# A two-layer encoder on one core: the Strassen subtractions of the down weights moved two chunks later and pinned behind a low part

## The chip, the core and the metric

The kernel runs on one core of a Trainium2 chip. The metric is the device time of one execution in microseconds (us); three runs of the kernel before took 2059.7, 2064.2 and 2067.19 us, with a median of 2064.2 us.

## The reference

The reference is an encoder trunk of two layers over 256 tokens of width 2048, all in float32. Each layer has a token mixer (attention in two variants) and a channel mixer, each between two RMS norms and added to the residual. The change lies in the channel mixer:

```python
def conv_glu(h, w_up, conv_w, conv_b, w_down):
    u = h @ w_up                                  # (256, 2048) @ (2048, 11264)
    gate, val = u[..., :D_FF], u[..., D_FF:]      # D_FF = 5632
    gate = depthwise_conv3(gate, conv_w, conv_b)
    return (jax.nn.gelu(gate, approximate=False) * val) @ w_down
```

## The kernel before

**Products in parts.** Every weight is multiplied as a high part plus a low part. A chunk is 128x1024 float32 numbers of a weight, 512 KB. SP loads it into one of four `raw` buffers (line 135). ACT casts it to the high part `whi` (line 157), DVE subtracts that from the chunk, which gives the low part `wlo` (line 152), and PE multiplies both with the activations. `whi` and `wlo` have five buffers each (`PARTED`), and `weights` makes the parts of a chunk two chunks before PE uses them and asks for its load up to four further ahead.

**Up projection** (`ffn`, `proj_t`). The 11264 columns are done in 11 groups of 512 gate columns and 512 value columns. Each half of a group takes 8 chunks; a chunk is eight pairs of a matmul with `whi` (line 231, 512 columns wide) and one with `wlo` (line 233, 256 wide). After each chunk `tick` advances the side jobs by one step each. When a half is done, ACT and DVE empty its four PSUM banks: for the gates lines 304, 305, 1112 to 1118 (convolution and gelu), for the values lines 304, 305, 1130, 1131 and 689, 690.

**Side job: block sums** (`block_sums`). The down projection later uses a Strassen form with seven products in place of eight, and for it needs differences of blocks of the down weights. From the second group on, a generator makes them for 20 pairs of weights in each layer, one pair (a *job*) in seven ticks, each tick being one step `q` from 0 to 6. A job loads its 128x2048 block in two halves (line 1154, at `q` 0 and 1) into one of two buffers that the jobs use in turn, makes three subtractions on DVE (`minus`, line 1141: one of 1024 columns and two of 512), and writes the two halves back to DRAM as `b` (line 1160). The wide subtraction stands at `q` 6 of the job itself, the two narrow ones at `q` 0 of the next job, and the write-back at its `q` 2 and 3. With the block sums running, seven chunks of up weights share the DMA with two loads and two write-backs of half a megabyte.

**What sets the order.** Nobody writes the order of an engine by hand here. When the program is built, each engine's instructions are put in a row that the engine then works off strictly in turn, waiting at each for its semaphores; within the dependences the building may move an instruction ahead of others. `issue_after`, which `behind` wraps, forbids that: what is issued inside it stays behind the named instruction. So a subtraction that waits for a load on DVE holds up every low part and every PSUM emptying behind it, and a load that waits on SP holds up every chunk behind it.

Of the kernel before, what the change touches and what calls it, by code (L numbers as in the profile page):

```python
# [58 lines left out]
class Model:  # L59
# [78 lines left out]
    def _split(self, i, parts=1, late=False):  # L138
        if i >= len(self.chunks) or i in self.made:
            return  # L140
        self._load(i)
        raw = self.loaded.pop(i)
        if i in self.spot:
            hi, lo = self.spot.pop(i)()
        else:
            hi = self.wp.tile([P, 1024], F32R, tag="whi", name="whi", bufs=PARTED)
            lo = self.wp.tile([P, 1024], F32R, tag="wlo", name="wlo", bufs=PARTED)
        n = raw.shape[-1] // parts

        def low(s=slice(0, raw.shape[-1])):  # L150
            nc = self.nc
            return nc.vector.tensor_tensor(out=lo[:, s], in0=raw[:, s], in1=hi[:, s].bitcast(F32), op=ALU.subtract)  # L152

        with self.behind(self.gate):
            for j in range(parts):
                s = slice(n * j, n * j + n)
                self.nc.scalar.copy(hi[:, s], raw[:, s])  # L157
                if not late:
                    low(s)
        self.made[i] = (hi, lo)  # L160
        if late:
            return low
# [972 lines left out]
    def block_sums(self, layer, sp):  # L1135

        nc, w = self.nc, self.a[f"w_down{layer}"]
        jobs = [(h, p) for h in range(2) for p in range(PAIRS[layer][h])]

        def minus(x, a, b, n=512):  # L1140
            nc.vector.tensor_tensor(out=x[:, a:a + n], in0=x[:, b:b + n] if n > 512 else x[:, a:a + n],  # L1141
                                    in1=x[:, a:a + n] if n > 512 else x[:, b:b + n], op=ALU.subtract)

        def half(x, i):
            return x[:, 1024 * i:1024 * i + 1024]

        old = None
        for n in range(len(jobs) + 1):
            job, new = (jobs[n] if n < len(jobs) else None), None
            for q in range(7):  # L1150
                if job and q == 0:
                    new = sp.tile([P, 2048], F32, tag=("st", "g_last")[n % 2], name="blocks", bufs=1)
                if job and q < 2:
                    nc.sync.dma_start(out=half(new, q), in_=half(w[job[0], job[1]], q))
                if old and q == 0:
                    minus(old[1], 1536, 512)
                    minus(old[1], 0, 1536)
                    kept = self.blocks[layer, *old[0]] = self.dram.tile([P, 2048], F32, name=f"b{layer}{old[0][0]}_{old[0][1]}")
                if old and q in (2, 3):
                    nc.sync.dma_start(out=half(kept, q - 2), in_=half(old[1], q - 2))  # L1160
                    if q == 3 and not job:
                        return
                if job and q == 6:
                    minus(new, 512, 1024, 1024)
                yield
            old = (job, new)

# [295 lines left out]
```

## Time and profile before

| | |
|---|---|
| median of three runs | 2064.2 us (2059.7 to 2067.19) |
| profiled execution | 2060.65 us, of which span 2058.9 us |
| PE matmul busy | 2037.1 us, 99% |
| PE weight loads busy | 1746.5 us, 85% |
| DVE busy | 1560.2 us, 76% |
| ACT busy | 1156.4 us, 56% |
| DMA, mean over the span | 248 GB/s |
| block sums run, layer 0 | from 343 to about 662 us |
| block sums run, layer 1 | from about 1339 to about 1663 us |

A line L231 of the profile is line 231 of the kernel; PEld is PE's loading of weights, SPq is SP's DMA queue. In a group of instructions the idle time is that of the engine just before them, with what ended it. The end of a matmul is modelled, so that a stall of PE can show partly as a longer matmul; the number of matmuls done in a stretch does not depend on that.

### The profile page before, as it was taken

What the parts mean: (1) busy time and instruction counts of PE and PEld (TensorE: products, weight loads), DVE (VectorE), ACT (ScalarE), POOL (GpSimd) and SP (SyncE); (2) the same over time, 40 slices, a digit from 0 to 9 for tenths busy, and PEclk for the clock granted to TensorE, in tenths of its full rate; (3) what the DMA queues carried; (4) which work ended last, traced back from release to release, by engine and by line L of the source; (5) the groups of instructions that cost most, each with busy time, mean ns of one, the idle gap of its engine ahead of it and who ended that gap; (6) DMA issues with size and microseconds to landing.
All of it is one profiled execution on the core that took longest, in us unless ns stands there. A gap on an engine that the chain in (4) does not pass through costs nothing.

```text
span 2058.9 us, 29791 instructions
## 1 busy us (share of the span) xinstructions
PE 2037.1 (99%) x10882; PEld 1746.5 (85%) x10882; DVE 1560.2 (76%) x2388; ACT 1156.4 (56%) x1817; POOL 0.2 (0%) x4
## 2 busy tenths in 40 slices
PE   9999999999999999999999999999999999999998
PEld 7888888888888888888878998888888888888886
DVE  6877757878777676977787875688887776688777
ACT  7655546554454555656665665565554555566664
POOL 0000000000000000000000000000000000000000
PEclk9999999999999999999999999999999999999999
DMA  9545567998998666788965445699899976668895
GB/s 334 180 152 161 166 198 245 318 321 308 331 305 310 208 182 192 237 295 280 317 204 180 141 129 170 207 321 334 311 316 306 316 252 195 192 198 303 271 321 197
DMA packets 145587, 509.75 MB, mean 248 GB/s; under 512 B 16160, under 2 KB 16672, under 8 KB 145440
## 3 DMA queue, kind: packets, MB, share of 16 engines
q1 hardware_dynamic: 145152, 507.58, 74.6%
q8 instruction: 85, 1.39, 0.3%
q14 instruction: 62, 0.51, 0.1%
q10 hardware_dynamic: 288, 0.28, 0.0%
HBM read 459.55 MB, written 48.23 MB: 247 GB/s over the span
## 4 chain that ended last, share of the span: by engine, by line
PE 87%; DVE 5%; DMA 4%; issue 2%; ACT 1%; SPq 0%; DVEq 0%; ACTq 0%
PE ps L231 25%; PE ps L233 12%; PE ps L216 8%; PE ps L214 8%; PE ps L215 8%; PE ps L1287 7%; PE ps L1286 7%; PE ps L1289 7%; DMA blocks<-in_w_down 3%; DVE wlo L152 2%; PE ps L641 1%; PE ps L300 1%; DMA raw<-in_w_up 1%; DVE blocks L1141 1%; PE ps L544 1%
## 5 line engine op out<-in xcount | busy, mean ns | idle before, releaser
L152 DVE TENSOR_TENSOR wlo<-raw,whi 128x1024 fp32r<-128x1024 f32 (+1 forms) x663 | 793.7, 1205 | 298.7 <-ACT whi L157 292.2
L157 ACT CAST whi<-raw 128x1024 fp32r<-128x1024 f32 (+1 forms) x663 | 682.9, 1036 | 520.7 <-PE ps L231 184.2
L231 PE MATMUL ps<-xhl,whi 128*128 128x512 f32 x2752 | 960.8, 396 | 0.0
L233 PE MATMUL ps<-xhl,wlo 128*128 128x256 f32 x2752 | 765.1, 280 | 8.7 <-DVE wlo L152 8.6
L231 PEld LDWEIGHTS ps<-xhl,whi 128*128 128x128 f32 x2752 | 516.5, 188 | 118.5
L233 PEld LDWEIGHTS ps<-xhl,wlo 128*128 128x128 f32 x2752 | 519.8, 189 | 15.6 <-DVE wlo L152 12.8
L1286 PE MATMUL ps<-whi,gh 128*128 128x512 f32 x440 | 171.5, 390 | 0.0
L1287 PE MATMUL ps<-whi,gl 128*128 128x512 f32 x440 | 171.4, 390 | 0.0
L1141 DVE TENSOR_TENSOR blocks<-blocks 128x512 f32<-128x512 f32 (+1 forms) x120 | 104.0, 867 | 85.1 <-DMA blocks<-in_w_down 55.3
L152 DVE TENSOR_TENSOR wlo<-raw_more,whi 128x1024 fp32r<-128x1024 f32 (+1 forms) x117 | 130.7, 1132 | 48.6 <-ACT whi L157 43.8
L157 ACT CAST whi<-raw_more 128x1024 fp32r<-128x1024 f32 (+1 forms) x117 | 113.2, 979 | 77.2 <-PE ps L1287 70.0
L1289 PE MATMUL ps<-wlo,gh 128*128 128x512 f32 x440 | 138.8, 390 | 0.0
L214 PE MATMUL ps<-whi,xhl 128*128 128x512 f32 x336 | 132.4, 395 | 1.7 <-ACT whi L157 1.7
L215 PE MATMUL ps<-wlo,xhl 128*128 128x512 f32 x336 | 131.6, 392 | 0.0
L216 PE MATMUL ps<-whi,xhl 128*128 128x512 f32 x336 | 131.1, 391 | 0.1
L304 ACT COPY gw<-ps 128x256 f32<-128x256 f32 x176 | 62.9, 368 | 93.7 <-DVE misc L305 43.2
L214 PE MATMUL ps<-whi,oh 128*128 128x512 f32 x256 | 100.4, 392 | 0.0
L215 PE MATMUL ps<-wlo,oh 128*128 128x512 f32 x256 | 99.8, 390 | 0.0
L216 PE MATMUL ps<-whi,ol 128*128 128x512 f32 x256 | 99.8, 390 | 0.0
L1286 PEld LDWEIGHTS ps<-whi,gh 128*128 128x128 f32 x440 | 82.6, 188 | 17.6 <-DVE ps L1171 0.4
L1289 PEld LDWEIGHTS ps<-wlo,gh 128*128 128x128 f32 x440 | 82.6, 188 | 17.3 <-DVE wlo L152 0.3
L1287 PEld LDWEIGHTS ps<-whi,gl 128*128 128x128 f32 x440 | 82.6, 188 | 17.0
(231 smaller groups left out, 2336.3 us busy)
## 6 DMA issues: line engine op xcount, KB each, us to landing
raw<-in_w_up SPq DMA_DIRECT2D x352, 512.0 KB, 4.9
raw<-in_w_in SPq DMA_DIRECT2D x88, 512.0 KB, 4.2
blocks<-in_w_down SPq DMA_DIRECT2D x80, 512.0 KB, 6.4
b<-blocks SPq DMA_DIRECT2D x80, 512.0 KB, 6.9
raw<-in_w_down SPq DMA_DIRECT2D x77, 512.0 KB, 5.2
raw<-in_w_out SPq DMA_DIRECT2D x64, 512.0 KB, 4.1
raw_more<-in_w_down SPq DMA_DIRECT2D x59, 512.0 KB, 5.7
raw<-b SPq DMA_DIRECT2D x42, 512.0 KB, 6.0
```

The lines of the kernel that those rows point to most:

```text
L152: return nc.vector.tensor_tensor(out=lo[:, s], in0=raw[:, s], in1=hi[:, s].bitcast(F32), op=ALU.subtract)
L157: self.nc.scalar.copy(hi[:, s], raw[:, s])
L214: mm(ps, lh, rh, start=start, stop=False)
L215: mm(ps, lh, rl, start=False, stop=False)
L216: return mm(ps, ll, rh, start=False, stop=stop)
L231: ins = mm(out[i], hi[:, s[kk]], x(k), start=k == 0, stop=False, skip_group_check=opening)
L233: ins = mm(out[i][:, :T], lo[:, s[kk]], x(k)[:, :T], start=False, stop=k == nk - 1, skip_group_check=opening)
L304: self.nc.scalar.copy(b, ps[:, T:])
L1141: nc.vector.tensor_tensor(out=x[:, a:a + n], in0=x[:, b:b + n] if n > 512 else x[:, a:a + n], in1=x[:, a:a + n] if n > 512 else x[:, b:b + ...
L1286: mm(bank, xh, w[0][:, c], start=start, stop=False, skip_group_check=loose)
L1287: mm(bank, xl, w[0][:, c], start=False, stop=False, skip_group_check=loose)
L1289: ins = mm(bank, xh, w[1][:, c], start=False, stop=stop, skip_group_check=loose)
```

## The change

The three subtractions of a job are moved to the steps `q` 1 (the wide one) and `q` 2 (the two narrow ones) of the next job, and each is issued behind the last low part that was made. The write-back moves from `q` 2 and 3 to `q` 3 and 4. `_split` keeps the instruction of the last low part in `self.low`. The loads stay at `q` 0 and 1, and nothing is added to or taken from the arithmetic. Lines behind line 1154 move down by two, and `minus` keeps line 1141.

```diff
                 self.nc.scalar.copy(hi[:, s], raw[:, s])
                 if not late:
-                    low(s)
+                    self.low = low(s)
...
                 if job and q < 2:
                     nc.sync.dma_start(out=half(new, q), in_=half(w[job[0], job[1]], q))
-                if old and q == 0:
-                    minus(old[1], 1536, 512)
-                    minus(old[1], 0, 1536)
+                if old and q == 1:
+                    with self.behind([self.low]):
+                        minus(old[1], 512, 1024, 1024)
+                if old and q == 2:
+                    with self.behind([self.low]):
+                        minus(old[1], 1536, 512)
+                        minus(old[1], 0, 1536)
                     kept = self.blocks[layer, *old[0]] = self.dram.tile([P, 2048], F32, name=f"b{layer}{old[0][0]}_{old[0][1]}")
-                if old and q in (2, 3):
-                    nc.sync.dma_start(out=half(kept, q - 2), in_=half(old[1], q - 2))
-                    if q == 3 and not job:
+                if old and q in (3, 4):
+                    nc.sync.dma_start(out=half(kept, q - 3), in_=half(old[1], q - 3))
+                    if q == 4 and not job:
                         return
-                if job and q == 6:
-                    minus(new, 512, 1024, 1024)
                 yield
```

The order of PE's row is the same in both kernels. Two places show what moves on the others.

On DVE, in layer 0, the emptying of the gate banks of the seventh group: before, the wide subtraction of a job stands in the middle of it (`blocks` is the job's buffer, `gw`, `yf` and `misc` are tiles of the emptying; in brackets are the semaphores that an instruction waits for, `DMAHW` those of a DMA).

```order
L152 TENSOR_TENSOR wlo<-raw,whi 128x1024 [waits DMAHW5_49,PE_49,Activation_49]
L305 TENSOR_TENSOR gw<-ps,gw 128x256 [waits Activation_49] x2
L1112 TENSOR_TENSOR gw<-gw,misc 128x256 [waits DVE_49] x2
L1141 TENSOR_TENSOR blocks<-blocks 128x1024 [waits DMAHW6_49,DMAHW3_49,DMAHW1_49]
L1114 SCALAR_TENSOR_TENSOR yf<-gw,gains,yf 128x255 [waits Activation_49] x2
L1116 SCALAR_TENSOR_TENSOR yf<-gw,gains,yf 128x255 [waits DVE_49] x2
L305 TENSOR_TENSOR gw<-ps,gw 128x256 [waits DVE_49,PE_49]
L305 TENSOR_TENSOR gw<-ps,gw 128x256 [waits DVE_49,Activation_49]
L1112 TENSOR_TENSOR gw<-gw,misc 128x256 [waits DVE_49] x2
L152 TENSOR_TENSOR wlo<-raw,whi 128x1024 [waits DMAHW7_49]
```

The same emptying on DVE in the changed kernel, and what follows it.

```order
L305 TENSOR_TENSOR gw<-ps,gw 128x256 [waits DVE_49]
L305 TENSOR_TENSOR gw<-ps,gw 128x256 [waits DVE_49,Activation_49]
L1112 TENSOR_TENSOR gw<-gw,misc 128x256 [waits DVE_49] x2
L152 TENSOR_TENSOR wlo<-raw,whi 128x1024 [waits DMAHW4_49,PE_49,Activation_49]
L1114 SCALAR_TENSOR_TENSOR yf<-gw,gains,yf 128x255 [waits Activation_49] x2
L1116 SCALAR_TENSOR_TENSOR yf<-gw,gains,yf 128x255 [waits DVE_49] x2
L152 TENSOR_TENSOR wlo<-raw,whi 128x1024 [waits DMAHW6_49,PE_49,Activation_49]
L1141 TENSOR_TENSOR blocks<-blocks 128x1024
L152 TENSOR_TENSOR wlo<-raw,whi 128x1024 [waits DMAHW0_49,PE_49,Activation_49]
L1141 TENSOR_TENSOR blocks<-blocks 128x512 [waits DVE_49]
L152 TENSOR_TENSOR wlo<-raw,whi 128x1024 [waits DMAHW1_49,PE_49,Activation_49]
L1141 TENSOR_TENSOR blocks<-blocks 128x512 [waits DVE_49]
```

The wide subtraction has left the emptying, stands behind a low part, and at this place waits for no DMA of its own. Counted over layer 0, the second load of a job stands on SP so that 2 to 4 low parts lie between it and the job's wide subtraction before (none for the last job), and 6 to 8 after (20 for the first two jobs).

On SP, in layer 0, before: the write-backs (L1160) of two jobs and the loads (L1154) of the next one, between the loads of up weights (L135).

```order
L135 DMA raw_5860<-in_w_up0 128x1024
L1160 DMA b01_6_6746<-blocks_6551 128x1024
L1160 DMA b01_7_6909<-blocks_6742 128x1024
L135 DMA raw_5883<-in_w_up0 128x1024
L135 DMA raw_5905<-in_w_up0 128x1024
L1154 DMA blocks_6905<-in_w_down0 128x1024
L135 DMA raw_5927<-in_w_up0 128x1024
L1154 DMA blocks_6905<-in_w_down0 128x1024
```

On SP in the changed kernel, the write-back of job 6 of the second half and the loads before it; the write-backs now have line 1164.

```order
L1164 DMA b01_5_6600<-blocks_6354 128x1024 x2
L135 DMA raw_6628<-in_w_up0 128x1024
L135 DMA raw_6651<-in_w_up0 128x1024
L135 DMA raw_6673<-in_w_up0 128x1024
L135 DMA raw_6723<-in_w_up0 128x1024
L1154 DMA blocks_6741<-in_w_down0 128x1024
L135 DMA raw_6747<-in_w_up0 128x1024
L1154 DMA blocks_6741<-in_w_down0 128x1024
L135 DMA raw_6771<-in_w_up0 128x1024
L135 DMA raw_6796<-in_w_up0 128x1024
L1164 DMA b01_6_6791<-blocks_6550 128x1024 x2
```

The loads of a job and the write-back of the job before it in the same buffer now keep a fixed distance: 2 to 5 loads of up weights lie between the first write-back and the first load into that buffer, where it was 1 to 8 before. In layer 0 the block sums were spread over 112 loads of up weights and are now spread over 157.

## The prediction

> **What bounds the kernel now.** I read the page first, then the waits of PE, then the rate of its matmuls by stretches.
>
> ```profile
> PE 2037.1 (99%) x10882; PEld 1746.5 (85%) x10882; DVE 1560.2 (76%) x2388; ACT 1156.4 (56%) x1817; POOL 0.2 (0%) x4
> ```
>
> PE is busy for 2037.1 of 2058.9 us of span, so only a PE that stalls less can make this kernel faster. The waits of PE and of its weight loads (engine, line, what it waited for; us in total, times, longest us), over the whole span and then in the stretches with block sums of layer 0 and layer 1:
>
> ```profile
> PE ps L233 <- DVE wlo L152: 8.6, 10, 2.4
> ...
> PEld ps L233 <- DVE wlo L152: 12.8, 13, 2.7
> ...
> PE ps L233 <- DVE wlo L152: 4.5, 5, 2.4
> ...
> PE ps L233 <- DVE wlo L152: 4.1, 5, 2.1
> ```
>
> All ten waits of PE for a low part, 8.6 us, lie in the two stretches with block sums (4.5 + 4.1), and the late engine is DVE. Now the rate: the matmuls of line 231 in windows (us from the span's start, length, PE busy with their count, PEld busy, granted clock, DMA share, GB/s).
>
> ```profile
> 360.00:480.00 120.00, 120.00 (x348) 65.03 (x347) 1.00 0.92 323
> 480.00:650.00 170.00, 163.75 (x466) 88.16 (x466) 0.99 0.90 313
> 660.00:820.00 160.00, 160.00 (x454) 85.22 (x453) 1.00 0.66 198
> 1360.00:1480.00 120.00, 120.00 (x347) 64.98 (x346) 1.00 0.92 324
> 1480.00:1650.00 170.00, 164.44 (x469) 88.68 (x468) 0.99 0.91 312
> 1660.00:1820.00 160.00, 160.00 (x462) 86.58 (x463) 1.00 0.66 199
> ```
>
> Undisturbed, 120 us hold 347 of these matmuls, 0.346 us each, or 2.77 us for a chunk of eight. At that pace 170 us hold 491.6. Layer 0 did 466 (25.6 too few, 8.9 us) and layer 1 did 469 (22.6 too few, 7.8 us). So the two layers lose 16.7 us, against 8.6 us of plain idle: the rest is in matmuls and weight loads stretched around a stall, as the 12.8 us of PEld show, and in the clock, below. 16.7 us is the most that the change can win where it acts. The 454 against 462 rows between 660 and 820 us are a slightly slower pace of this execution (8 x 0.346 = 2.8 us) with no block sums near, which I leave alone.
>
> The two largest stalls, in order of time (start, duration, engine, line; in brackets the idle time before and what ended it):
>
> ```profile
> 628.82 0.75 DVE L1112 TENSOR_TENSOR gw<-gw,misc 128x256 f32<-128x256 f32 x2
> 633.24 1.23 DVE L1141 TENSOR_TENSOR blocks<-blocks 128x1024 f32<-128x1024 f32 x1 [3.66 <-DMA blocks<-in_w_down]
> ...
> 637.30 1.22 DVE L152 TENSOR_TENSOR wlo<-raw,whi 128x1024 fp32r<-128x1024 f32 x1
> ...
> 638.57 0.53 PE L233 MATMUL ps<-xhl,wlo 128*128 128x256 f32 x1 [2.38 <-DVE wlo L152]
> ...
> 1628.53 1.23 DVE L1141 TENSOR_TENSOR blocks<-blocks 128x1024 f32<-128x1024 f32 x1 [3.99 <-DMA blocks<-in_w_down]
> ...
> 1633.86 0.39 PE L233 MATMUL ps<-xhl,wlo 128*128 128x256 f32 x1 [2.15 <-DVE wlo L152]
> ```
>
> DVE stood 3.66 us at the wide subtraction, because the job's load had not landed, then had to finish a piece of the emptying; the low part ended at 638.5 and PE, which had waited 2.38 us, went on at 638.57. Layer 1's longest stall (3.99 us on DVE, 2.15 us on PE) has the same shape.
>
> **The change part by part.** The subtractions by form on DVE from 480 to 650 us, and the wide one from 1480 to 1650 us (count | busy us, mean ns | idle us before, by releaser):
>
> ```profile
> L1141 DVE TENSOR_TENSOR blocks<-blocks 128x512 f32<-128x512 f32 x22 | 15.1, 688 | 0.3
> L1141 DVE TENSOR_TENSOR blocks<-blocks 128x1024 f32<-128x1024 f32 x10 | 12.3, 1226 | 30.2 <-DMA blocks<-in_w_down 14.3 <-DMA raw<-in_w_up 8.1 <-issue 7.8
> ...
> L1141 DVE TENSOR_TENSOR blocks<-blocks 128x1024 f32<-128x1024 f32 x10 | 12.3, 1225 | 30.3 <-DMA blocks<-in_w_down 20.4 <-issue 6.2 <-DMA raw<-in_w_up 3.7
> ```
>
> *The wide subtraction, later and pinned.* Ten of them keep DVE idle for 30 us in each layer's disturbed stretch, 3 us each; the narrow ones wait for nothing. The DMA's own times (KB, median us to landing; then the spread of the loads and write-backs of `blocks` together):
>
> ```profile
> raw<-in_w_up SPq DMA_DIRECT2D x352, 512.0 KB, 4.9
> ...
> blocks<-in_w_down SPq DMA_DIRECT2D x80, 512.0 KB, 6.4
> b<-blocks SPq DMA_DIRECT2D x80, 512.0 KB, 6.9
> ...
> DMA to landing us min/median/max: 3.4/6.6/10.3
> ```
>
> Before, 2 to 4 low parts lie between a job's second load and its wide subtraction, 5.5 to 11 us at 2.77 us each: about as long as a load takes (6.4 median, 10.3 at most). After, it is 6 to 8, 16.6 to 22 us, and the longest landing fits 1.6 times. The 30 us of idle DVE therefore go in each layer, and with them what they cause on PE.
>
> *The work itself stays:* per job 1.226 + 2 x 0.688 = 2.6 us of DVE. It now stands between low parts, so a low part comes at most 1.2 us later for it, or 2.6 us where all three meet; the parts are made two chunks (5.5 us) ahead of PE, which covers that. DVE is not short of time on the whole (start, length, PE, PEld, DVE busy, ACT, POOL, clock, DMA):
>
> ```profile
> 360.00:480.00 120.00, 120.00 (x695) 104.94 (x694) 99.28 (x157) 65.08 (x99) 0.00 (x0) 1.00 0.92 323
> ```
>
> In this quiet stretch DVE is busy for 99.28 of 120 us with the same subtractions in it, and PE keeps the pace that it has without them (160 us for 462 matmuls in layer 1, 0.346 us). If the cover fails at a bank emptying, small stalls stay: eight of the ten waits are small and sum to 8.6 - 2.4 - 2.1 = 4.1 us. I keep half of that as not gone, 2 us. The bounds are 0 and 6.7 us: all 4.1, stretched as the 14.0 us that the stalls cost (16.7 less 2.7 for the clock, below) are to 8.6.
>
> *The pin* adds no wait of its own: it is order on one engine, and the row it pins to stands on the same DVE. What is queued behind a pinned subtraction is the next low part.
>
> *Half clock.* Two windows of the whole trace within the up projections have a granted clock of 0.51; the third row is the stretch right after the first (matmuls of both lines, x12, x14 and x21):
>
> ```profile
> 638.60:642.10 3.50, 3.50 (x12) 3.02 (x13) 3.50 (x6) 2.25 (x4) 0.00 (x0) 0.51 0.86 260
> 1635.30:1638.80 3.50, 3.50 (x14) 2.97 (x13) 3.50 (x5) 1.53 (x3) 0.00 (x0) 0.51 0.94 341
> 642.10:645.60 3.50, 3.50 (x21) 3.04 (x21) 3.45 (x5) 1.05 (x1) 0.00 (x0) 1.00 0.90 336
> ```
>
> They lose 9/21 and 7/21 of 3.5 us, 1.5 + 1.2 = 2.7 us, which is part of the 16.7. The first begins at 638.6, when PE has just stood 2.38 us, and the second follows within 2 us of the other longest stall. I take them for consequences of the stalls, so they go too. [...]
>
> *The loads on SP.* Loads and write-backs are as many as before and stay on SP. A load now stands 2 to 5 chunk loads behind the first write-back from its buffer (1 to 8 before) and must wait until that has landed: 2 x 2.77 = 5.5 us against 6.9 median and 10.3 at most, so SP stands 1.4 to 4.8 us at some of them, with chunk loads behind it. Before, this was
>
> ```profile
> SPq L1154 <- DMA b<-blocks: 27.9, 14, 8.0
> ```
>
> 27.9 us in 14 waits, up to 8.0. How much delay is hidden takes the cast on ACT too (count | busy us, mean ns):
>
> ```profile
> L157 ACT CAST whi<-raw 128x1024 fp32r<-128x1024 f32 (+1 forms) x663 | 682.9, 1036 | 520.7 <-PE ps L231 184.2
> ```
>
> Four `raw` buffers and five pairs of parts lie between a chunk's load and PE; I take them as at least five chunks of lead, 13.8 us by the pace above; less 4.9 for landing and 2.3 for the two parts (1.04 ACT, 1.22 DVE), an estimated 6.6 us of delay are hidden, and 4.8 fit. I set it at nothing (bounds 0 and the slower rival). One load for the down stage, of the first `b`, moves up in layer 0 and waits on SP for that write-back: once, at most 10.3 us, hidden in the same way but for some 3.7 us at worst.
>
> *The DMA's rate.* Seven chunks now carry 7 + 2 + 2 = 11 transfers of 0.524 MB in 19.4 us: 297 GB/s, under the 323 that it delivers in the windows above; before, 5.6 chunk loads a job meant 9.6 transfers in 15.5 us, 325, so the DMA was full. The block sums end 45 chunk loads later, ten chunk loads (27.7 us) ahead of the first load of down weights, against 10.3 us for the slowest landing: nothing waits.
>
> **Sum.** 16.7 - 2.0 = 14.7 us off the profiled execution's 2060.65, which gives 2046. That execution lies 3.5 us below the median of 2064.2; how much of this is other stalls of the same kind cannot be seen, and I carry half of it, 1.8: **2048 us**.
>
> **The rivals.**
>
> *Half clock stays*, because something other than PE's stalls sets the two windows: 14.0 - 2 = 12 us less, 2060.65 - 12 + 1.8 = 2050.5. For it: the windows lie 996.7 us apart, as a clock-driven event might; against it: each meets one of the two longest stalls. Chance 0.10. [...]
>
> *DVE is simply too full at the emptyings*, and all eight small stalls stay: gain 16.7 - 6.7 = 10.0, so 2052.5. For it: the small ones cluster at emptyings; against it: none from 360 to 480 us. Chance 0.13.
>
> *Nothing moves:* the DMA is the real limit, and when DVE no longer waits for `blocks`, ACT waits for `raw` with the same stalls. For it: a DMA share of 0.9 in the stretch; against it: the demand falls to 297 GB/s. 2061 to 2064. That the change doesn't do what it says is excluded by the order, where the wide subtraction has moved. Chance 0.13.
>
> *Slower:* SP standing behind write-backs uses up the lead of the chunk loads at each of the 36 handovers of a buffer (18 a layer). It decides from a delay above some 6.6 us. If PE then stood 0.65 us each time, 36 x 0.65 = 23.4 us against 14.7 won: 2060.65 + 8.7 = 2069. For it: landings up to 10.3 us and the shortest distance of 5.5 us; against it: 8.0 us of waiting on SP at once in the trace without a stall that starts from a chunk load. Chance 0.07.
>
> **How the numbers follow.** The forecast has the remaining 0.57. About 0.3% (6.2 us) is what a measurement of this kernel can tell from no change, so faster means below 2058.0. Forecast, half clock and full DVE all lie below it, 0.80 together; I take 0.03 off for their upper ends, 0.77. Nothing moves gives 0.13 and 0.02 of those ends, 0.15, for the same, and the slower rival 0.07 and the other 0.01, 0.08. The range begins at 2042 (all 16.7 us gone, and the slow pace's 2.8 us as well: 2041) and ends at 2059, past the upper ends of the three faster cases; it leaves out the slower rival and most of nothing moves.
>
> **What would show it.** Right: the wide subtraction's idle time on DVE near nothing, line 233's wait for the low part under 2 us in all, the granted clock 1.00 through both up projections, 491 matmuls of line 231 in 170 us of either disturbed stretch. Wrong: ACT's wait for `raw` grown from its present sum and PE still waiting (nothing moves), SP's wait of L1154 for `b` far above 27.9 us with late chunk loads (slower), a clock of 0.5 without a stall before it (half clock).

## The result and the profile after

The changed kernel takes 2040.67 us (median of four runs, 2040.63 to 2042.25), the kernel before 2063.88 us (median of four runs, 2059.7 to 2067.19): a ratio of 0.989, with a 95% interval of 0.9872 to 0.9909. The forecast was 2048 us, and the time lies below the low end of its range, 2042. The profiled execution took 2040.68 us, 20.0 less than the profiled 2060.65 of before.

The page of the changed kernel: busy times, then the chain that ended last, by engine.

```profile
PE 2025.8 (99%) x10882; PEld 1740.6 (85%) x10882; DVE 1562.1 (77%) x2388; ACT 1161.3 (57%) x1817; POOL 0.2 (0%) x4
...
PE 98%; DVE 1%; ACT 1%; DMA 0%; issue 0%; DVEq 0%; SPq 0%
```

The matmuls of line 231 in the changed kernel, in the two disturbed stretches and in the quiet one between 660 and 820 us (columns as in the prediction).

```profile
480.00:650.00 170.00, 170.00 (x491) 91.91 (x491) 1.00 0.85 298
660.00:820.00 160.00, 159.99 (x462) 86.44 (x461) 1.00 0.79 265
1480.00:1650.00 170.00, 170.00 (x492) 92.01 (x491) 1.00 0.85 298
```

The 491 matmuls that the prediction asked for are there, in both layers, at a clock of 1.00. The stretch from 660 to 820 us, which the prediction left alone, has gone from 454 to 462 as well. The groups of the low matmuls and of the subtractions:

```profile
L233 PE MATMUL ps<-xhl,wlo 128*128 128x256 f32 x2752 | 757.5, 277 | 0.0
...
L1141 DVE TENSOR_TENSOR blocks<-blocks 128x512 f32<-128x512 f32 (+1 forms) x120 | 103.8, 865 | 0.7
```

PE no longer waits for a low part at all, and DVE stands 0.7 us in 120 subtractions. Before, the same row was

```profile
L1141 DVE TENSOR_TENSOR blocks<-blocks 128x512 f32<-128x512 f32 (+1 forms) x120 | 104.0, 867 | 85.1 <-DMA blocks<-in_w_down 55.3 <-issue 16.9 <-DMA raw<-in_w_up 11.8
```

Two rows answer to the rivals: SP's wait at the loads of `blocks`, and ACT's for chunks.

```profile
SPq L1154 <- DMA b<-blocks: 69.8, 29, 4.1
```

```profile
ACT whi L157 <- DMA raw<-in_w_up: 41.3, 21, 5.0
```

SP stands longer in sum than before (27.9), but 4.1 us at most, and PE waits for nothing behind it. ACT's wait for chunks has fallen (it was 72.0 us), and did not take the place of DVE's.

### The profile page after: what moved, and what is told of

It is laid out like the page before. It is cut to its first block, busy times and chain, and to the rows that moved or that the text cites. A ratio compares the mean times of both kernels' runs of the same rounds, so it can differ in the third digit from the quotient of the medians.

```text
span 2038.9 us, 29776 instructions
## 1 busy us (share of the span) xinstructions
PE 2025.8 (99%) x10882; PEld 1740.6 (85%) x10882; DVE 1562.1 (77%) x2388; ACT 1161.3 (57%) x1817; POOL 0.2 (0%) x4
## 4 chain that ended last, share of the span: by engine, by line
PE 98%; DVE 1%; ACT 1%; DMA 0%; issue 0%; DVEq 0%; SPq 0%
PE ps L231 31%; PE ps L233 16%; PE ps L216 8%; PE ps L214 8%; PE ps L215 8%; PE ps L1289 7%; PE ps L1288 7%; PE ps L1291 7%; PE ps L641 2%; PE ps L300 1%; PE ps L544 1%; DMA raw<-in_w_in 0%; PE ps L471 0%; PE ps L551 0%; ACT whi L157 0%
## 5 line engine op out<-in xcount | busy, mean ns | idle before, releaser
L233 PE MATMUL ps<-xhl,wlo 128*128 128x256 f32 x2752 | 757.5, 277 | 0.0
L152 DVE TENSOR_TENSOR wlo<-raw_more,whi 128x1024 fp32r<-128x1024 f32 (+1 forms) x117 | 130.6, 1131 | 48.9 <-ACT whi L157 44.1
```

The lines of the kernel that those rows point to most:

```text
L233: ins = mm(out[i][:, :T], lo[:, s[kk]], x(k)[:, :T], start=False, stop=k == nk - 1, skip_group_check=opening)
```

## What the stretch was short of

One row that the prediction did not read turns out to be the one that matters: how long DVE, between 480 and 650 us, waits for the cast, that is, has nothing to do. Before:

```profile
DVE wlo L152 <- ACT whi L157: 4.8, 5, 2.1
```

After:

```profile
DVE wlo L152 <- ACT whi L157: 33.2, 30, 2.8
```

The page's 76% of DVE is a mean over the whole kernel. Here, before, DVE was busy for 134.1 of 170 us and stood 30.5 us at the subtractions; with 4.8 us left over, it was the engine that set the pace. (A *stand* here is time in which DVE waits at a subtraction with the rest of its row behind it; a *stall* is PE waiting for a low part.) The low parts show it: at best one is ready some 9 us before the first matmul of line 233 that reads it (start of that matmul less end of the low part, in the rows of the trace). Taken over eight chunks at a time, that largest lead falls in layer 0 of the kernel before, from 432 to 612 us, through 8.9, 7.1, 7.9, 6.0, 6.5, 5.7, 4.3 to 3.9 us. In the changed kernel, but for the first eight chunks of a layer, the largest is 8.4 or more in every eight and the smallest never under 3.6. So PE's ten stalls were not ten separate collisions at emptyings. One came early, at 499.78 us, behind the longest stand of all (6.15 us); before the others the lead had been used up slowly. What all ten have in common is a stand of the wide subtraction, of 2.0 to 6.2 us, which ended less than 10 us before. An emptying is not needed: between this stand and its stall there is none.

```profile
604.07 1.95 DVE L1141 TENSOR_TENSOR blocks<-blocks 128x1024 f32<-128x1024 f32 x2 [4.34 <-DMA raw<-in_w_up]
605.94 1.22 DVE L152 TENSOR_TENSOR wlo<-raw,whi 128x1024 fp32r<-128x1024 f32 x1
...
607.21 0.39 PE L233 MATMUL ps<-xhl,wlo 128*128 128x256 f32 x1 [0.63 <-DVE wlo L152]
```

Earlier stands of up to 3.2 us, from 397 to 463 us, had stalled nothing.

This account is a second theory, formed after the result. I call it the budget: a stand on DVE costs nothing until, together with all other work of the stretch, it exceeds DVE's spare time. The theory of the prediction, which I call the distance, says that a load that comes late makes DVE stand, and the stand stalls PE. The experiments below had to tell these apart, and both from the rate of the transfers, which the pin also lowers.

## The experiments

**Built only.** With the steps moved as in the change but without the pin, the rows of all five engines are the same as before the change. They are the same, too, when the jobs of the kernel before are given nine steps in place of seven. Without a pin these changes of the steps decide nothing: the building moves the jobs ahead all the same.

**The pin without the move** (edit to the changed kernel).

```diff
-                if old and q == 1:
-                    with self.behind([self.low]):
-                        minus(old[1], 512, 1024, 1024)
-                if old and q == 2:
+                if old and q == 0:
                     with self.behind([self.low]):
                         minus(old[1], 1536, 512)
...
-                if old and q in (3, 4):
+                if old and q in (2, 3):
...
+                if job and q == 6:
+                    with self.behind([self.low]):
+                        minus(new, 512, 1024, 1024)
```

> The subtractions keep the steps of the kernel before (the wide one at q 6 of its job, the narrow ones at q 0 of the next, the write-back at q 2 and 3), and each is pinned behind the last low part; nothing else changes. Theory (the stalls came from DVE standing at the wide subtraction until its load landed, and any distance over a landing cures it): in layer 0, 4 to 9 low parts now lie between the second load and the wide subtraction, 11 to 25 us against a slowest landing of 9.1 us, so the subtraction waits under 2 us in all, PE has no wait for a low part, and the time is that of the changed kernel, 2040.7 us within 2. Rival (the two chunks of delay do the work, the pin only keeps them): the distances of 4 are too short for the slow landings, DVE stands again, and a third or more of the 23 us comes back, 2048 us or above.

2040.70 us, ratio 0.9884 (0.986 to 0.9909), no wait of PE for a low part. The pin gives everything; the two chunks give nothing more.

**The loads later, two low parts before the wide subtraction** (edit to the changed kernel).

```diff
-                if job and q < 2:
-                    nc.sync.dma_start(out=half(new, q), in_=half(w[job[0], job[1]], q))
+                if job and q in (4, 5):
+                    with self.behind([self.fetched]):
+                        nc.sync.dma_start(out=half(new, q - 4), in_=half(w[job[0], job[1]], q - 4))
```

> The changed kernel, but each job's loads are issued at q 4 and 5 and pinned behind the last chunk load, so that 2 low parts lie between the second load and the wide subtraction, the commonest distance of the kernel before; the order of DVE stays that of the changed kernel, with the subtractions behind low parts. Theory (waiting for the load): the wide subtraction stands on DVE for a landing of about 6 us less 2 x 2.77, so 0.5 to 3 us each, 20 to 100 us over the 40 jobs, PE waits for low parts again, and 3 to 20 us of the gain are lost: 2044 to 2060 us. Rival (it was the subtraction's place inside the emptying of the banks that cost, not the load): no more than 2 us are lost, 2040.7 to 2042.7 us, even if DVE stands.

2041.26 us, ratio 0.9886 (0.9866 to 0.9907). DVE hardly stood (0.4 us for a load): from the second load's issue to the wide subtraction there were 6.0 to 13.7 us, median 10.7, where the kernel before had 7.0 and the changed one has 23.7. The number of low parts between them did not make the stand that I wanted, so the run leaves the distance untested.

**One chunk shorter still**: the same with the loads at steps 5 and 6 and the subtractions at 0 and 1 of the next job.

> The changed kernel with the loads of a job moved to its steps 5 and 6, each pinned behind the last chunk load, and the subtractions to steps 0 and 1 of the next job, still pinned behind the last low part: 0 to 2 low parts lie between the second load and the wide subtraction, so DVE must stand. Theory (the short distance alone makes the loss): DVE idle at the wide subtraction 2 to 5 us in each of 40 jobs, 80 to 200 us in all, PE waits for low parts again, 8 to 60 us in all, and the time is 2048 to 2100 us. Rival (it is the place within an emptying that costs; between two low parts the lead of two chunks covers a stand of 5 us): the same idle time on DVE, PE's wait under 2 us, 2040 to 2043 us.

```profile
DVE blocks L1141 <- DMA blocks<-in_w_down: 31.4, 14, 5.1
```

2041.0 us, ratio 0.9904 (0.9869 to 0.994). DVE stands up to 5.1 us at once, longer than the two stands ahead of the longest stalls of the kernel before (3.66 and 3.99 us, though not than its longest, 6.15), and PE does not wait once. The stands sum to 39.2 us, where it was 85.1. So a long stand alone costs nothing, and the theory of the distance cannot be the whole cause.

**Only the wide subtraction pinned; only the narrow ones pinned.** In each the other `with self.behind([self.low]):` is taken away.

> The changed kernel with only the wide subtraction pinned; the narrow ones are free to be moved ahead as far as the wide one. Theory (only the wide subtraction waits for a load, so its pin is all that counts): 2040 to 2043 us, no wait of PE for a low part. Rival (the narrow ones, where they fall into an emptying, make small stalls of their own): four or more small waits of PE, 2044 to 2055 us.

> The changed kernel with only the narrow subtractions pinned; the wide one is free and stands again 0 to 4 low parts behind the job's second load. Theory: as the kernel before, idle time of DVE at the wide subtraction 40 to 70 us, PE waits for low parts 5 to 12 us, 2055 to 2066 us. Rival (the narrow ones, two in an emptying, carried half or more of the loss): 2041 to 2051 us.

2041.06 us (0.9871 to 0.9942) and 2040.17 us (0.985 to 0.9934). The second was expected to be as slow as the kernel before. Its wide subtraction is free, is moved ahead as before, and stands:

```profile
DVE blocks L1141 <- DMA blocks<-in_w_down: 20.8, 13, 3.6
```

but only 20.8 us in all, against 55.3, and PE never waits. On SP its jobs come one in seven chunk loads, against one in 5.6 before. Any one pin ties the jobs to their steps, so two things had changed at once: the stands, and how densely the jobs stand.

**Jobs of five steps**, pinned and with a long distance: denser than before, without a stand.

```diff
-            for q in range(7):
+            for q in range(5):
...
-                if old and q == 1:
+                if old and q == 0:
...
-                if old and q == 2:
+                if old and q == 1:
...
-                if old and q in (3, 4):
+                if old and q in (2, 3):
```

> The changed kernel with jobs of five steps in place of seven (loads at 0 and 1; the pinned subtractions at 0 and 1 and the write-back at 2 and 3 of the next job): five chunk loads and four transfers of blocks in 13.9 us ask the DMA for 340 GB/s, more than the 327 that any window of the kernel before reached, while DVE has time and little to stand for. New theory (DVE's spare time is a budget: in the changed kernel it waited 33 us of 170 for the cast, and PE stalls only when what DVE stands or does besides uses that up, as the 30 us of the kernel before did): 2040 to 2044 us, with no wait of PE for a low part. Rival (the rate of the jobs fills the DMA; the pin helped because it holds them at one in seven chunks): ACT waits for raw over 100 us and PE stalls, 2048 to 2070 us.

2044.36 us, ratio 0.9913 (0.9886 to 0.9939). By the medians the density by itself costs 3.7 us of the 23; the theory's number was just missed, the rival's by more. The profile is that of the slowest of the four executions (2050.51 us): 329 GB/s and all 492 matmuls of line 231 from 480 to 650 us, 0.8 us of stands in the whole run, and a single stall of PE, 1.81 us at 653.84 us. Behind it come a window at half clock and then the slower of two paces, 472 matmuls from 650 to 820 us in place of 491; both are taken up below.

**No distance**, at one job in seven chunks: loads at steps 5 and 6, the wide subtraction at 6.

> The changed kernel with the loads of a job at its steps 5 and 6, each behind the last chunk load, and the wide subtraction at step 6 too, the narrow ones at step 0 of the next job, all pinned: one chunk less than in the run with the shorter distance, where DVE stood 31.4 us in all and PE never. I expect DVE to stand 60 to 140 us in all. Budget theory: no loss while it stays under some 76 us a layer (33 of 170 us, over 388 us of block sums): 2040 to 2045 us. Rival (a stand of 3.6 us or more stalls PE wherever it meets an emptying, as the two longest of the kernel before): 5 to 12 us of waits of PE for low parts, 2048 to 2062 us.

```profile
L1141 DVE TENSOR_TENSOR blocks<-blocks 128x512 f32<-128x512 f32 (+1 forms) x120 | 103.8, 865 | 72.7 <-DMA blocks<-in_w_down 66.7 <-issue 5.4
```

2044.75 us, ratio 0.9907 (0.9882 to 0.9932), and 1.5 us of waits of PE. Stands of 72.7 us, nearly the 85.1 of the kernel before, cost 4 us here and 23 there (by the medians): it is not the stands' sum alone either.

**DVE work added**: in the changed kernel, during the block sums, two or four of every seven low parts are made twice (the second keeps PE's row in its order).

```diff
+            self.extra = [self.at + i for i in range(20, 160) if i % 7 in (0, 3)]
...
-                    self.low = low(s)
+                    for _ in range(2 if i in self.extra else 1):
+                        self.low = low(s)
```

> The changed kernel with DVE work added during the block sums: of every seven chunks two have their low part made twice, 2.4 us of DVE in 19.4 us, or 21 us in 170. Budget theory: less than the 33 us that DVE has, so nothing: 2040 to 2043 us, no wait of PE for a low part. Rival (each piece of 1.2 us that falls into an emptying costs): PE waits 4 us or more for low parts, 2046 to 2060 us.

> As the run before, with four of every seven low parts made twice (PE's row kept in the order that it has without them): 4.9 us of DVE in 19.4 us, or 43 us in 170, against the 33 us that it has. Budget theory: DVE lacks 9.5 us in 170, about 22 us over the 388 us of a layer's block sums, less the some 9 us by which low parts are ahead of PE: 13 us a layer, 2067 us (2055 to 2085). Rival (only single long stands matter, not the sum): 2040 to 2046 us.

2042.5 us (ratio 0.99, 0.9876 to 0.9924) and 2108.89 us (1.0224, 1.0192 to 1.0256). In the second, PE's waits for low parts over the whole span, and then DVE's waits for the cast from 480 to 650 us:

```profile
PE ps L235 <- DVE wlo L153: 43.2, 34, 3.4
```

```profile
DVE wlo L153 <- ACT whi L158: 8.7, 8, 2.5
```

Twice the added work is not twice the loss but, by the medians, 68 us against 2. That is a budget with an edge. The size was off: 26 us were expected, with the 33 us that DVE waits for the cast taken as all usable. With two more, in a profiled execution of 2046.09 us (the slowest of four), 17.4 us of waiting for the cast were left in the stretch and PE already waited 3.0 us in the whole run.

**The subtractions on POOL**, otherwise the kernel before.

```diff
-            nc.vector.tensor_tensor(out=x[:, a:a + n], in0=x[:, b:b + n] if n > 512 else x[:, a:a + n],
+            nc.gpsimd.tensor_tensor(out=x[:, a:a + n], in0=x[:, b:b + n] if n > 512 else x[:, a:a + n],
```

> The kernel before with the three subtractions of a job on POOL in place of DVE; steps, loads and write-backs stay as before, one job in 5.6 chunk loads, and nothing is pinned, so any stand for a load is now POOL's. Budget theory (the kernel before lost what DVE stood and did beyond its spare time): no wait of PE for a low part, 2040 to 2044 us. Rival (the rate of the jobs, 325 GB/s asked of the DMA, makes chunk loads late): PE waits for low parts 4 to 12 us, 2050 to 2066 us.

2070.57 us, slower than before (1.0055, 1.0036 to 1.0075), with 16.2 us of waits of PE. Both theories missed. DVE's rows from 480 to 650 us, of the kernel with POOL:

```profile
L152 DVE TENSOR_TENSOR wlo<-raw,whi 128x1024 fp32r<-128x1024 f32 x58 | 84.4, 1472 | 27.8 <-ACT whi L157 26.4 <-PE ps L231 1.4
...
L1130 DVE TENSOR_TENSOR misc<-misc 128x256 f32<-128x256 f32 x12 | 13.8, 1189 | 0.0
...
L305 DVE TENSOR_TENSOR gw<-ps,gw 128x256 f32<-128x256 f32 x16 | 5.9, 409 | 0.0
```

Before they took 1222, 422 and 417 ns. With POOL subtracting, the low parts take 1.2 times as long in the mean and line 1130 2.8 times, while line 305, which reads PSUM, is unchanged. Of the rows of lines 1112, 1130, 1131 and of the low parts (each with two inputs in SBUF) that began during a subtraction of POOL, 84 of 99 are longer, and each of the 84 ends no earlier than that subtraction. Apart from POOL none of lines 1112, 1130 and 1131 took over 425 ns; beside it they took up to 2641. The 33 rows of line 305 beside it took 420 at most. The run therefore says nothing on the rate of the transfers.

**Both together**, five steps and no distance, and **no subtractions at all**: the kernel before with an empty `minus`, so that the down projection gets blocks that are not subtracted.

> Jobs of five steps with no distance: loads at steps 3 and 4, each behind the last chunk load, the wide subtraction at step 4 and the narrow ones at step 0 of the next job, all pinned. It has the rate of the run with five steps (3.7 us slower than the changed kernel, no stand on DVE) and the stands of the run with no distance (4 us slower, 72 us of stands). Budget theory (stands and the denser jobs draw on the same spare time of DVE): more than some 13% of DVE's time is drawn on, as in the kernel before, and the losses are more than their sum: 2055 to 2075 us, PE waits for low parts 6 us or more. Rival (two separate small losses, and the kernel before lost its 23 us in another way): 2045 to 2051 us.

> The kernel before with the three subtractions of the jobs left out, so that the down projection gets blocks that are not subtracted; loads and write-backs keep their number and their places on SP. Budget theory: DVE has neither the stands nor the 2.6 us a job, PE never waits for a low part, 2040 to 2043 us. Rival (the rate of the transfers, 325 GB/s asked, makes the chunk loads late, and so the low parts): the waits for raw stay at 60 us or more and PE still waits, 2048 to 2064 us.

The first: 2050.2 us, ratio 0.9931 (0.9915 to 0.9948). The stands that it was built for did not come (9.2 us in all); ACT waited 169.8 us for chunks instead, and SP 115.6 us at write-backs for subtractions. It falls in the rival's range, but its premise failed, and it decides nothing. The second: 2040.84 us, ratio 0.9887 (0.9872 to 0.9901). Its windows (all engines; columns as in the prediction) and ACT's wait for chunks:

```profile
480.00:650.00 170.00, 170.00 (x982) 148.65 (x981) 118.02 (x190) 92.62 (x142) 0.00 (x0) 1.00 0.95 331
```

```profile
ACT whi L157 <- DMA raw<-in_w_up: 5.8, 5, 2.0
```

The DMA now delivers 331 GB/s, more than the 313 of the kernel before, with as many loads and write-backs of blocks (in layer 0 from 343 to 643 us, where it was to 661; on SP some stand a few places off), and chunk loads are hardly ever late. The rate of the transfers is excluded. The late chunks of the kernel before (72.0 us of ACT's waits) were then a consequence of DVE's lateness; the likely way, not tried by itself, is that a `raw` buffer comes free when DVE has made its low part (SP's waits for that are its largest: 1065.4 us in the kernel before, 1017.9 in the changed one). This run also gives the budget: without the jobs DVE is busy for 118.0 of 170 us, so 52.0 are spare.

What the jobs and the additions drew from those 52 us between 480 and 650 us (the subtractions' busy and idle time; for the two rows of added work the growth of DVE's busy time over the run without subtractions), and what was left as waiting for the cast. These columns are read from the profiled execution, so its own time stands beside them, and then the median:

| kernel | drawn, us | left, us | profiled execution, us | median, us |
|---|---|---|---|---|
| no subtractions | 0 | 53.5 | 2040.65 | 2040.84 |
| changed | 22.0 + 0.1 | 33.2 | 2040.68 | 2040.67 |
| one chunk shorter | 21.9 + 3.8 | 29.5 | 2041.31 | 2041.0 |
| only the narrow ones pinned | 20.7 + 7.3 | 28.1 | 2040.87 | 2040.17 |
| five steps | 29.7 + 0.2 | 22.5 | 2050.51 | 2044.36 |
| no distance | 20.8 + 12.9 | 21.9 | 2046.58 | 2044.75 |
| five steps and no distance | 31.1 + 0.8 | 20.8 | 2050.91 | 2050.2 |
| two more low parts of seven | 34.0 | 17.4 | 2046.09 | 2042.5 |
| four more low parts of seven | 38.9 | 8.7 | 2109.24 | 2108.89 |
| before | 27.4 + 30.5 | 4.8 | 2060.65 | 2063.88 |

With 28 us or more left nothing is lost; between 17 and 23 us the profiled executions lose 5 to 10 us; under 9 us it is 20 and more. The row of four more draws little only because PE had already slowed down, and did 442 pairs of matmuls there (885 rows of both lines) against 491. The order of neighbouring rows is not strict, and the columns are of layer 0: in layer 1 two more low parts of seven left only 13.8 us, and PE did its 492 matmuls. So I claim the edge and not a formula.

The kernel with POOL does not fit and is left out: it had 26.4 us left and was 30 us slower than the changed kernel all the same, and its emptyings had become longer one by one (line 1130 took 1189 ns for 422 in the mean). There the lead tells what the waits for the cast do not: its largest value in eight chunks was 3.2 to 4.9 us all the way from 476 to 642 us. That the longer emptyings used it up was not tried by itself.

**Stalls on purpose.** Two runs of the changed kernel with ten holds each: at one chunk in every second group the low part (1223 ns in the mean in the changed kernel from 480 to 650 us) is made many times more, and PE's row is kept in order around it.

```diff
+            self.extra = {self.at + 16 * g + 7: n for g, n in zip((1, 3, 5, 7, 9), ((7, 8, 9, 10, 11), (9, 10, 11, 12, 13))[layer])}
...
-                    self.low = low(s)
+                    for _ in range(1 + self.extra.get(i, 0)):
+                        self.low = low(s)
```

> The changed kernel with ten deliberate holds of DVE: at one chunk in groups 2, 4, 6, 8 and 10 of each layer the low part is computed again 7 to 11 times (layer 0) and 9 to 13 times (layer 1), about 1.13 us each, and the matmuls of that chunk and the five behind it are kept in program order. The low part is some 9 us ahead of PE, so PE should stand between 0 and about 6 us, more with each step. Theory A (half clock is a consequence of a stall): every stall of over about 2.2 us is followed within 3.4 us by a window of some 3.4 us at half clock, and none under 1 us is. [...] Theory B (after a stall PE falls into one of two paces, 346.7 or 353.3 ns a pair, and keeps it until the next one): the stretches between stalls have either pace and nothing between, at least one of the ten has the slow one, and no stretch changes pace without a stall. Rival B (the slow pace of 650 to 832 us in the kernel before had nothing to do with stalls): all stretches at 346.7 ns, or changes of pace in mid-stretch. Time: 2040.7 us, and ten stalls of 0 to 6 us, 25 to 40 us together with the half clocks: 2060 to 2085 us.

> The changed kernel with ten deliberate holds of PE again, shorter ones: at one chunk in each of five groups per layer the low part is made 4 to 5.5 further times on DVE (in halves). From the first set of holds (7 to 13 further times, stalls of 3.8 to 13.3 us, half clock for 6.8 to 17.1 us after each) I expect stalls of about 0 to 4 us here. Theory A (half clock follows any stall that fills more than about half of one of the 3.41 us windows, so from some 2 us on): stalls of 2.2 us or more are followed by 3.4 us or more at 0.5, those under 1.5 us by none. [...] Theory B (two paces of the matmuls, 346.7 and 353.3 ns a pair, chosen anew at each stall and kept to the next): every stretch between two stalls has one of the two and nothing else, some three in ten the slow one, small stalls too. Rival B (slow pace only follows half clock): stretches behind a stall without half clock are all at 346.7 ns.

The first took 2154.34 us and had ten stalls of 3.8 to 13.3 us, each with half clock behind it; the second 2053.07 us, with stalls of up to 3.0 us and no half clock behind any, although the longest, 2.98 us, exceeds the two of the kernel before that have it (2.38 and 2.15). So theory A is wrong as it stands. The half-clock records begin and end on a grid of 3.413 us (in the kernel before they begin at 638.65 and 1635.34 us, 292 such steps apart, and last one step each), so I laid that grid over the traces (in the run of the shorter holds the records at its start and end give the grid). The kernel before, the window ahead of each half clock and that of the half clock in layer 0:

```profile
635.20:638.60 3.40, 1.02 (x7) 0.62 (x5) 3.40 (x9) 2.34 (x5) 0.00 (x0) 1.00 1.00 404
638.60:642.00 3.40, 3.40 (x11) 2.92 (x12) 3.40 (x6) 2.25 (x4) 0.00 (x0) 0.51 0.85 254
...
1631.90:1635.30 3.40, 1.45 (x8) 1.31 (x9) 3.40 (x9) 2.25 (x4) 0.00 (x0) 1.00 0.76 276
```

The shorter holds: the longest stall, and the windows of it, which the grid cuts in two, and of the next longest.

```profile
667.82 0.39 PE L237 MATMUL ps<-xhl,wlo 128*128 128x256 f32 x1 [2.98 <-DVE wlo L153]
```

```profile
663.10:666.50 3.40, 1.73 (x10) 1.22 (x8) 3.35 (x4) 1.04 (x1) 0.00 (x0) 1.00 0.86 275
666.50:669.90 3.40, 2.08 (x12) 1.87 (x13) 2.13 (x5) 0.74 (x2) 0.00 (x0) 1.00 0.94 337
669.90:673.30 3.40, 3.40 (x22) 2.99 (x21) 3.23 (x7) 2.93 (x6) 0.00 (x0) 1.00 0.77 305
...
755.30:758.70 3.40, 1.54 (x9) 1.10 (x7) 3.40 (x4) 1.04 (x1) 0.00 (x0) 1.00 0.44 161
758.70:762.10 3.40, 3.23 (x18) 2.86 (x19) 3.40 (x8) 1.58 (x4) 0.00 (x0) 1.00 0.83 245
```

A stall of 2.98 us that the grid cuts in two has no half clock behind it, and one of 2.15 us that falls almost whole into a window has one. On the exact grid, over the traces of all runs here, every full-clock window in which PE is busy for 1.49 us or less is followed by one at half clock, and none with 1.68 us or more is. In between there is no sharp edge: the window of 755.30 above (1.55 us on the exact grid) is not followed by one, but the window of the single stall of the run with five steps (1.60 us, a stall of 1.81 us) is:

```profile
651.40:654.80 3.40, 1.59 (x9) 1.06 (x8) 3.40 (x5) 1.81 (x2) 0.00 (x0) 1.00 0.62 253
654.80:658.20 3.40, 3.40 (x13) 3.01 (x12) 3.40 (x4) 0.00 (x0) 0.00 (x0) 0.50 0.80 235
```

On the pace, theory B held. The matmuls of line 235 (line 231 of the changed kernel) between stalls of the shorter holds, 80 us each, none with half clock:

```profile
486.00:566.00 80.00, 80.00 (x232) 43.16 (x231) 1.00 0.86 307
576.00:656.00 80.00, 80.00 (x228) 42.61 (x227) 1.00 0.87 295
670.00:750.00 80.00, 80.00 (x232) 43.20 (x231) 1.00 0.82 288
```

Pairs of matmuls came every 346.7 or every 353.3 ns, and each stretch kept its pace to the next stall: slow behind a stall of some 0.6 us, fast again behind the one of 2.98 us. In the longer holds three of ten stretches were slow. I found no rule for which comes.

## Why the prediction was right and wrong

- **Right: the sign and the first sum.** The 16.7 us between 480 and 650 us and between 1480 and 1650 us came back in full (491 and 492 matmuls), the wide subtraction no longer stands, and the work itself is hidden.
- **Wrong: "If the cover fails at a bank emptying, small stalls stay", 2 us.** None stayed. The step took the eight small waits for local collisions at emptyings, from a quiet window in which DVE had time ("DVE is not short of time on the whole"). In the disturbed stretch it had 4.8 us left of 170, and the small stalls, like the large ones, each came behind a stand. With the stands gone they lose their cause too.
- **Wrong: the slow pace, "which I leave alone".** The 454 matmuls between 660 and 820 us were the slower of the two paces, entered at a stall of the block sums and kept to the next stall. The 2.8 us were part of the price of the stalls. 14.7 + 2.0 + 2.8 = 19.5 of the 20.0 us measured.
- **Wrong: 1.8 us for the median.** The profiled run of before lay 3.2 us under the median of its four runs; that of the changed kernel lies on its own. The executions of each kernel without stalls agree to within 2.6 us, and those of before in this study spread from 2052.72 to 2074.03; that a kernel with stalls gets other clock windows and another pace each time is my estimate from these spreads, and was not shown. The medians differ by 23.2 us and the profiles by 20.0. How much of the spread is pace and how much is clock was not measured.
- **These three terms are the miss.** 2047.8 less 2.0, 2.8 and 1.8 is 2041.2, and 2040.67 was measured. The range began at 2042 although its own sentence has 2041 for all 16.7 us gone and the slow pace with them; that is the case that came.
- **Right, though for a narrower reason: the half clock went with the stalls**, and the rival that it stays was wrong. In the traces it went by how a stall lay on the grid: the 2.98 us that the grid cuts in two had no half clock behind them, the 2.15 us almost whole in one window had.
- **The distance of 6 to 8 low parts** removes the stands as forecast, but it was not needed: one chunk shorter, with stands of up to 5.1 us at once, the time is the same. What the pin does for the time is to tie the jobs to their steps, one in some seven chunk loads, which thins both the stands and the subtractions until DVE has time again.
- **The rivals.** Full DVE at the emptyings was the nearest to the cause of the loss, but was given as something that would stay, and as tied to emptyings: two of the small stalls (607.21 and 622.04 us) have no emptying between their stand and PE's wait. Nothing moves was wrong: the transfers' rate is excluded by the run without subtractions, whose 331 GB/s also show that the DMA was not full at the 325 that the prediction works out. Slower was wrong: SP stood 69.8 us, 4.1 at most, within the delay that was held to be hidden.

What stays open: how the loss of the kernel before divides between its stands and its denser jobs. By the medians density alone costs 3.7 us and stands alone some 4. That most of the 23 comes from having both is argued from this and not shown: in the run that was to have both, DVE hardly stood.

## What to carry to other kernels

Read an engine's spare time in the stretch that loses, by its waits for its own supplier and by the lead of its product over the consumer, and not from its share of the page: what it stands and what it does draw on the same time, and a loss begins where that is gone, not at the first stand. If an order is made by a builder that moves free instructions ahead, check whether a step's place has any effect at all, since here only the pin had. And a stall's price includes what it leaves behind, here a slower pace until the next stall (454 matmuls of line 231 in 160 us in place of 462).

## Not expected of the hardware

- In the traces of these runs half clock followed every full-clock window of the 3.413 us grid in which PE was busy for 1.49 us or less, and none with 1.68 us or more; a stall of 1.81 us had it behind it and one of 2.98 us did not.
- The same matmul stream ran at two steady paces, 346.7 and 353.3 ns a pair, 1.9% apart at a full clock. Which one ran changed at some stalls, even at one of some 0.6 us, and then stayed until the next.
- With POOL subtracting, 84 of the 99 DVE rows of the low parts and of lines 1112, 1130 and 1131 that began beside it took longer, line 1130 2.8 times in the mean (422 to 1189 ns); the kernel with POOL's help was 0.55% slower than the one whose DVE stood.
